# Score products of a differential attention: the low part of the queries laid out over all 128 rows

## The chip, the cores and the metric

The kernel runs on one core of a Trainium2 chip. The metric is the device time of one execution in microseconds (us). All inputs lie in HBM at the start; the result is written back to HBM. Several runs of the kernel before were timed, and one execution of it was taken apart by the hardware profiler.

## The reference

One layer of a diffusion backbone works on 512 latent tokens and 256 context tokens of width 1024: a SwiGLU half step, then a mixer (gated linear attention and differential attention side by side, gated and added), then a second SwiGLU half step and a norm. What the change touches is the differential attention of the latent tokens:

```python
def _diff_block(q, k, v, lam):
    s = jnp.einsum('bqhcd,bkhcd->bhcqk', q, k).astype(jnp.float32) * (DIFF_DH ** -0.5)
    p = jax.nn.softmax(s, axis=-1)
    a = p[:, :, 0] - lam * p[:, :, 1]
    return jnp.einsum('bhqk,bkhe->bqhe', a.astype(v.dtype), v)
```

There are 8 heads. Each has two components c = 0, 1 of width 64, and 512 queries meet 768 keys (512 latent, 256 context). Queries and latent keys are turned by an axial rotary embedding first.

## The kernel before, in words

**Number format.** A matmul here takes operands in a reduced float32 format. To keep accuracy each operand is split into a high part (`...h`, a copy in the reduced format) and a low part (`...l`, the value minus the high part). A weight product is the sum of three matmuls: high by high, high by low and low by high.

**Stages.** First SwiGLU (to about 600 us), mixer (attention to about 975 us, gated linear attention and output projection after it), second SwiGLU. The attention goes by units `un` of two heads. While unit `un - 1` attends, the projections of unit `un` are woven in: `weave` takes the generator `attend` and a list of projection calls, and after each `yield` of the one runs the next of the other. In the last unit the projections of the mixing gates (`mgate`) take that place. Before the first unit stands a prologue: the query projections of heads 0 and 1 (`gemm_lat([0, 1], G)` and `diff_q`, L664 and L665), two `mgate` calls (L666, L667), the norm of the context tokens (L668 to L671), then the keys and values of heads 0 and 1.

**Queries.** `diff_q` (L546) gets the projected queries of one head (128 rows: rows 0 to 63 are component 0, rows 64 to 127 component 1; 512 tokens along the row). `rope` leaves the rotated values in a tile of tag `t1`, of which there are two buffers; `mgate` (L472) uses the same two buffers for its result, and so does the rope of the keys. ScalarE copies them to `qh` (L551), VectorE makes `ql` (L552). Four transfers on the SyncE queue (L555) copy each 64-row half of `qh` to both halves of the rows of `QQ[:, c, :]`, so that `QQ[:, c, :]` holds the high part of component c twice. `ql` stays as it is: component c in its own 64 rows.

**Keys.** `diff_k` (L558) makes `kr` (rotated), `kh` and `kl`, and copies them (L570, L571) to `KK[:, c, :]`: the high part of component c in the rows of c, its low part in the other 64 rows.

**Scores.** `score(i)` (L602) takes 128 queries of a head. For each component c it fills one score tile `sp` of 128 x 768 in PSUM by four matmuls (L611 to L614): `ql` of component c (64 rows) against `KK[r, c]` for 512 and then 256 keys, then `QQ[:, c]` (128 rows) against `KK[:, c]` for 512 and then 256 keys. The second pair gives high by high plus high by low in one pass, the first one low by high. A head has 4 blocks of queries, so there are 8 x 4 x 2 = 64 such groups of four. After each group VectorE takes the row maximum (L615) and ScalarE the exponential (L616). `flip` transposes the weights of the block before on TensorE (L633), ScalarE and VectorE split them (L636, L637), `value` multiplies them with the values. The score tiles and the transposes share two PSUM buffers (`big`).

**What sets the order.** The kernel is written as a dataflow program; when it is compiled, a planner simulates it with costs of its own, gives each tile a buffer and fixes the order of the instructions on each engine. Each engine and the SyncE queue then run their lists strictly in that order. Loads of weights (`wload`, L109: transfer to `raw`, copy to `whi` on ScalarE, subtraction to `wlo` on VectorE or GpSimd) are traced at a higher priority and also stand on the SyncE queue. The rest of the prologue that matters: the results of `gemm_lat` lie in two PSUM buffers (`gm`), which also take the key and value projections.

Of the kernel before, what the change touches and what calls it, by code (L numbers as in the profile page):

```python
# [10 lines left out]
F32 = mybir.dt.float32  # L11
# [45 lines left out]
def layer(tc, a, out, dump=None, stop=None):  # L57
# [49 lines left out]
    loaded = [None]  # L107

    def wload(src, w=1024, eng=None, hold=None):  # L109
        """hold: the pool and number of weights that stay."""  # L110
        pl, n, wt = (*hold, w) if hold else (wp, WB, 1024)
        raw = wp.tile([P, 1024], F32, tag="raw", name=u("raw"), bufs=RB)
        hi = pl.tile([P, wt], F32R, tag="whi", name=u("whi"), bufs=n)
        lo = pl.tile([P, wt], F32R, tag="wlo", name=u("wlo"), bufs=n)
        with tc.high_priority(offset=WPRI):
            SY.dma_start(raw[:, :w], src)
            S.activation(hi[:, :w], raw[:, :w], AF.Copy)  # L117
            ld = (eng or V).tensor_tensor(lo[:, :w], raw[:, :w], hi[:, :w].bitcast(F32), op=ALU.subtract)  # L118
        loaded[0] = ld.ins
        return hi, lo  # L120
# [35 lines left out]
    class Rms:  # L156
# [4 lines left out]
        def square(self):  # L161
            """where the next squares go; the last ones are left to the sums of finish()."""
            self.c += 1
            if self.c == 1:
                return self.acc
            self.sq = self.p.tile([P, self.n], F32, tag="sq", name=u("sq"), bufs=2)
            return self.sq
# [7 lines left out]
        def add2(self, ap, ap2):  # L175
            """two token ranges; the squares of the second one are left to GpSimd."""
            n = ap.shape[-1]
            sq = self.square()
            S.activation(sq[:, :n], ap, AF.Square)
            G.tensor_tensor(sq[:, n:], ap2, ap2, op=ALU.mult)  # L180
            if 1 < self.c < KT:
                for sl in (slice(0, n), slice(n, self.n)):
                    V.tensor_tensor(self.acc[:, sl], self.acc[:, sl], sq[:, sl], op=ALU.add)

        def scale(self, start=None):
            """1/rms, tokens on the partitions."""
            nt = self.n // P
            pv = sm(u("pv"))
            with tc.issue_after(start) if start else ExitStack():
                for t in range(nt):  # L190
                    for i, q in enumerate((self.acc, self.sq)):
                        PE.matmul(pv[:, t:t + 1], q[:, t * P:(t + 1) * P], ones[:, 0:1], start=i == 0, stop=i == 1)
            v = self.p.tile([P, nt], F32, tag="rv", name=u("v"), bufs=2)
            y = self.p.tile([P, nt], F32, tag="ry", name=u("y"), bufs=2)
            V.tensor_scalar(v, pv[:, :nt], 1.0 / D, EPS, op0=ALU.mult, op1=ALU.add)
            newton(self.p, y, v, [P, nt], "nw")
            return y

        def finish(self, R, start=None, after=None):
            """R: the psum, or a function that gives the psum of a token tile.  # L200

            start: the instruction ahead of the sums; after: work ahead of R.
            """
            if not callable(R):
                R = lambda t, R=R: R[:, t * P:(t + 1) * P]
            nt = self.n // P
            y = self.scale(start)
            with tc.issue_after(after()) if after else ExitStack():
                for t in range(nt):
                    dg = self.p.tile([P, P], F32, tag="dg", name=u("dg"), bufs=3)  # L210
                    V.tensor_scalar(dg, ident, y[:, t:t + 1], None, op0=ALU.mult)
                    mm = PE.matmul(R(t), ones, dg, start=True, stop=True)
            return mm.ins

    def mod_h(pool_, x_, R, k, m, i, ai, hh, hl):
        """one feature tile of the modulated norm, as hi and lo parts."""
# [7 lines left out]
    class Parts:  # L224
        """hi (0) and lo (1) parts of feature-major tokens: latent tiles, and a tile for the context."""
# [15 lines left out]
    def mm_k(dst, w, h, k, segs):  # L241
        """the products of one feature tile; dst(o0, n): psum slice for a token segment."""
# [10 lines left out]
    class Ffn:  # L253
# [5 lines left out]
        def psum(self):  # L259
            """psum of the two up projections of one f tile: functions of a token segment."""  # L260
# [33 lines left out]
        def down(self, f0, nf, m, parts, w=None):  # L294
            """parts: (x slice, token offset, tokens, gate)."""
# [10 lines left out]
        def run(self, first, parts, extra=None):  # L306
            """all f tiles from first on and all but the last chunk of the down projection."""
# [16 lines left out]
    # ================= FFN 1 =================  # L324
# [104 lines left out]
    # last chunk of the down projection: latent tokens first, so that their norm runs under the context part  # L429
# [25 lines left out]
    # ================= mixer =================  # L455
# [4 lines left out]
    def gemm_lat(blks, eng=None):  # L460
        """128-column blocks of W_in for the latent tokens, the feature tiles outermost."""
# [7 lines left out]
    def mgate(pool_, tag, j, eng=None):  # L469
        """tanh of half of a tile of the mixing gates, kept in DRAM."""  # L470
# [9 lines left out]
    def gemm_fm(blk):  # L480
        """128 columns of W_in, feature-major: (latent psum, context psum)."""
# [7 lines left out]
    def tm_items(blk, nt, consume):  # L489
        """256 columns of W_in, token-major, two token tiles a bank: a call for each bank."""  # L490
# [40 lines left out]
    with tc.tile_pool(name="dqp", bufs=1) as dq:  # L531
# [14 lines left out]
        def diff_q(pl):  # L546
            qh = dq.tile([P, TL], F32R, tag="qh", name=u("qh"), bufs=1)
            ql = dq.tile([P, TL], F32R, tag="ql", name=u("ql"), bufs=3)
            QQ = dq.tile([P, 2, TL], F32R, tag="QQ", name=u("QQ"), bufs=3)
            qr = rope(pl, None, 0.125)  # L550
            S.activation(qh, qr, AF.Copy)  # L551
            V.tensor_tensor(ql, qr, qh.bitcast(F32), op=ALU.subtract)  # L552
            for c in range(2):
                for d in range(2):
                    SY.dma_start(QQ[d * 64:(d + 1) * 64, c, :].bitcast(F32), qh[c * 64:(c + 1) * 64, :].bitcast(F32))  # L555
            return QQ, ql

        def diff_k(blk):  # L558
# [3 lines left out]
            kl = dp.tile([P, T], F32R, tag="kl", name=u("kl"), bufs=1)  # L562
# [4 lines left out]
            V.tensor_tensor(kl, kr, kh.bitcast(F32), op=ALU.subtract)  # L567
            for c in range(2):
                r, o_ = slice(c * 64, (c + 1) * 64), slice((1 - c) * 64, (2 - c) * 64)
                SY.dma_start(KK[r, c, :].bitcast(F32), kh[r, :].bitcast(F32))  # L570
                SY.dma_start(KK[o_, c, :].bitcast(F32), kl[r, :].bitcast(F32))  # L571
            return KK

        def diff_items(un, st):
            """the projections of a pair of heads, a list of calls that fill st."""
# [22 lines left out]
        def attend(un, st):  # L598
            """attention of a pair of heads; yields where other work should follow on the tensor engine."""
            vh, vl = st["v"]  # L600

            def score(i):  # L602
                QQ, ql = st[f"q{i // 4}"]
# [4 lines left out]
                for c in range(2):  # L608
                    sp = big(u("S"))
                    r = slice(c * 64, (c + 1) * 64)  # L610
                    for n0, n1 in ((0, TL), (TL, T)):  # L611
                        PE.matmul(sp[:, n0:n1], ql[r, qs], KK[r, c, n0:n1], start=True, stop=False)  # L612
                    for n0, n1 in ((0, TL), (TL, T)):
                        PE.matmul(sp[:, n0:n1], QQ[:, c, qs], KK[:, c, n0:n1], start=False, stop=True)  # L614
# [69 lines left out]
        def head_sums(un):  # L684
            """sums of squares of the heads of a pair, tokens on the partitions."""
# [40 lines left out]
    def branch(br, j, th, yhl):  # L726
        """one feature tile of a gated branch; the second one adds to the first and is split again."""
# [14 lines left out]
    # prefix sums of the log decays (times tau), one zero ahead of each chunk  # L742
# [11 lines left out]
    # head norms of the attention output  # L754
# [18 lines left out]
    # low-rank gate: stacked hi and lo parts  # L773
# [90 lines left out]
    with tc.tile_pool(name="glp", bufs=1) as gp:  # L864
        IT = 1.0 / 16.0

        def gla_core(hd, st, tail):
# [4 lines left out]
            # factors against the states: queries (fwd, bwd), keys (fwd, bwd; latent then context)  # L872
# [43 lines left out]
            def factors(hf):  # L916
                # factors of the binary split: at half size h the two halves of a 2h block meet at its middle
# [104 lines left out]
        for hd in range(GH):  # L1022
            if hd < GH - 1:
                nst, its = gla_items(hd + 1)
            else:
                its = [lambda j=j: mgate(gi, "q", j) for j in range(10, 16)]
                its.insert(3, lambda: None)
                # the branch of the attention takes the place of the tokens
# [94 lines left out]
    # ================= FFN 2 and the final norm =================  # L1123
# [49 lines left out]
def _fm(w, n):  # L1173
    """[D, n*128] -> n blocks [128, 8*128], contraction on the partitions."""
# [3 lines left out]
def _w2(w):  # L1178
    """[FF, D] -> [128, FF*8]: by chunk of f tiles, then output tile, then f tile."""
# [8 lines left out]
def arrange(inp):  # L1188
# [40 lines left out]
    # tables that depend on shapes alone  # L1229
# [32 lines left out]
```

## Time and profile before

| what | value |
|---|---|
| median of 3 runs | 1810.89 us |
| lowest and highest run | 1808.08, 1811.19 us |
| span of the profiled execution, first to last instruction | 1809.3 us |
| TensorE busy | 1763.3 us, 97% of the span |
| VectorE, ScalarE, GpSimd busy | 1000.8, 629.8, 111.5 us |
| TensorE share of the chain that ended last | 89% |

The profile gives the profiled execution by its span; the median of the runs is 1.6 us above it. PE is TensorE's matmul side, PEld its weight-load side; matmuls overlap in the pipeline and their ends are modelled, so that the distance from one matmul's start to the next one's start says more than the duration of one. DVE is VectorE, ACT ScalarE, POOL GpSimd, SP SyncE, SPq its queue of transfers. The attention's score products run from 663 to 964 us of the span.

### The profile page before, as it was taken

What the parts mean: (1) busy time and instruction counts of PE and PEld (TensorE: products, weight loads), DVE (VectorE), ACT (ScalarE), POOL (GpSimd) and SP (SyncE); (2) the same over time, 40 slices, a digit from 0 to 9 for tenths busy, and PEclk for the clock granted to TensorE, in tenths of its full rate; (3) what the DMA queues carried; (4) which work ended last, traced back from release to release, by engine and by line L of the source; (5) the groups of instructions that cost most, each with busy time, mean ns of one, the idle gap of its engine ahead of it and who ended that gap; (6) DMA issues with size and microseconds to landing.
All of it is one profiled execution on the core that took longest, in us unless ns stands there. A gap on an engine that the chain in (4) does not pass through costs nothing.

```text
span 1809.3 us, 24815 instructions
## 1 busy us (share of the span) xinstructions
PE 1763.3 (97%) x10184; PEld 1525.2 (84%) x10184; DVE 1000.8 (55%) x1666; ACT 629.8 (35%) x940; POOL 111.5 (6%) x190
## 2 busy tenths in 40 slices
PE   6999999999999999999999989999999999999998
PEld 4788888888888788888877889998888988888887
DVE  5554354354445856766655675767645743333435
ACT  3321121121113435555565543434423332222233
POOL 3100000000001300000000031212001200000000
PEclk9999999999999999999999899999999999999999
DMA  8333344243333532312222121112444222323231
GB/s 327 138 117 98 114 157 131 73 160 121 107 117 105 156 94 74 101 54 76 94 70 90 33 70 56 39 47 94 157 148 142 89 82 93 105 83 110 87 110 66
DMA packets 59426, 189.42 MB, mean 105 GB/s; under 512 B 7976, under 2 KB 8232, under 8 KB 58032
## 3 DMA queue, kind: packets, MB, share of 16 engines
q1 hardware_dynamic: 59312, 187.83, 32.2%
q8 instruction: 80, 1.31, 0.3%
q14 instruction: 34, 0.28, 0.0%
HBM read 168.93 MB, written 8.39 MB: 98 GB/s over the span
## 4 chain that ended last, share of the span: by engine, by line
PE 89%; DVE 3%; ACT 1%; issue 1%; DMA 1%; POOL 1%; DVEq 0%; ACTq 0%; POOLq 0%
PE h L249 21%; PE h L246 11%; PE pl L249 8%; PE dn L123 5%; PE dn L124 5%; PE dn L125 5%; PE pl L246 4%; PE pb L249 3%; PE ptm L504 3%; PE ptm L505 3%; PE ptm L506 3%; PE S L614 2%; PE S L612 2%; PE po L249 2%; PE pb L246 1%; PE pc L249 1%
## 5 line engine op out<-in xcount | busy, mean ns | idle before, releaser
L117 ACT ACTIVATE whi<-raw 128x1024 fp32r<-128x1024 f32 (+2 forms) x246 | 241.2, 984 | 505.9 <-PE dn L125 191.6
L118 DVE TENSOR_TENSOR wlo<-raw,whi 128x1024 fp32r<-128x1024 f32 (+2 forms) x231 | 262.2, 1137 | 220.7 <-ACT whi L117 219.2
L246 PE MATMUL h<-hH,wlo 128*128 128x512 f32 (+1 forms) x704 | 273.3, 388 | 1.9 <-ACT hH L221 1.4
L249 PE MATMUL h<-hL,whi 128*128 128x512 f32 (+1 forms) x704 | 274.5, 390 | 0.6 <-DVE hL L222 0.6
L249 PE MATMUL h<-hH,whi 128*128 128x512 f32 (+1 forms) x704 | 273.2, 388 | 0.0
L249 PE MATMUL h<-hC,whi 128*128 128x256 f32 x704 | 196.9, 280 | 0.0
L123 PE MATMUL dn<-gh,wlo 128*128 128x512 f32 (+1 forms) x568 | 194.5, 343 | 1.1 <-ACT gh L286 0.9
L124 PE MATMUL dn<-gl,whi 128*128 128x512 f32 (+1 forms) x568 | 194.1, 342 | 0.0
L125 PE MATMUL dn<-gh,whi 128*128 128x512 f32 (+1 forms) x568 | 193.6, 341 | 0.0
L246 PEld LDWEIGHTS h<-hH,wlo 128*128 128x128 f32 x704 | 132.2, 188 | 33.3 <-ACT hH L221 2.4
L249 PEld LDWEIGHTS h<-hH,whi 128*128 128x128 f32 x704 | 132.3, 188 | 29.6
L249 PEld LDWEIGHTS h<-hL,whi 128*128 128x128 f32 x704 | 132.2, 188 | 28.0 <-DVE hL L222 0.8
L246 PE MATMUL pl<-hH,wlo 128*128 128x512 f32 x328 | 132.2, 403 | 7.8 <-DVE sg L839 4.7
L285 DVE TENSOR_TENSOR g<-s,h 128x512 f32<-128x512 f32 (+2 forms) x46 | 36.2, 791 | 182.4 <-PE h L249 110.0
L249 PEld LDWEIGHTS h<-hC,whi 128*128 128x128 f32 x704 | 133.0, 189 | 0.6 <-DVE hC L222 0.4
L249 PE MATMUL pl<-hL,whi 128*128 128x512 f32 x328 | 130.9, 399 | 0.0
L249 PE MATMUL pl<-hH,whi 128*128 128x512 f32 x328 | 130.3, 397 | 0.0
L123 PEld LDWEIGHTS dn<-gh,wlo 128*128 128x128 f32 x568 | 107.6, 189 | 14.2 <-ACT gh L286 1.1
L125 PEld LDWEIGHTS dn<-gh,whi 128*128 128x128 f32 x568 | 107.5, 189 | 12.4
L124 PEld LDWEIGHTS dn<-gl,whi 128*128 128x128 f32 x568 | 107.6, 190 | 12.2
L505 PE MATMUL ptm<-wlo,hH 128*128 128x256 f32 x384 | 110.5, 288 | 5.0 <-DVE wlo L118 5.0
L504 PE MATMUL ptm<-whi,hL 128*128 128x256 f32 x384 | 111.9, 292 | 0.0
(269 smaller groups left out, 3339.9 us busy)
## 6 DMA issues: line engine op xcount, KB each, us to landing
raw<-win SPq DMA_DIRECT2D x65, 512.0 KB, 3.6
adaw<-ada SPq DMA_DIRECT2D x56, 512.0 KB, 4.4
raw<-f1w SPq DMA_DIRECT2D x44, 512.0 KB, 3.6
raw<-f2w SPq DMA_DIRECT2D x44, 512.0 KB, 3.5
aw<-ada SPq DMA_DIRECT2D x8, 1024.0 KB, 10.0
raw<-wbr SPq DMA_DIRECT2D x16, 512.0 KB, 3.9
raw<-f1w SPq DMA_DIRECT2D x16, 384.0 KB, 3.1
raw<-wout SPq DMA_DIRECT2D x12, 512.0 KB, 3.5
```

The lines of the kernel that those rows point to most:

```text
L117: S.activation(hi[:, :w], raw[:, :w], AF.Copy)
L118: ld = (eng or V).tensor_tensor(lo[:, :w], raw[:, :w], hi[:, :w].bitcast(F32), op=ALU.subtract)
L123: PE.matmul(out_, wl, xh, start=first, stop=False)
L124: PE.matmul(out_, wh, xlo, start=False, stop=False)
L125: PE.matmul(out_, wh, xh, start=False, stop=last)
L246: PE.matmul(dst(o0, n), wl[:, ks], h.at(0, k, o0, n), start=(k == 0), stop=False)
L249: mm = PE.matmul(dst(o0, n), wh[:, ks], h.at(i, k, o0, n), start=False, stop=(k == KT - 1 and i == 0))
L285: self.mark = V.tensor_tensor(g[:, sl], s[:, sl], pts[1][:, sl], op=ALU.mult).ins
L504: PE.matmul(o_, tl, wh[:, cs], start=f, stop=False)
L505: PE.matmul(o_, th, wl[:, cs], start=False, stop=False)
L506: PE.matmul(o_, th, wh[:, cs], start=False, stop=l)
L612: PE.matmul(sp[:, n0:n1], ql[r, qs], KK[r, c, n0:n1], start=True, stop=False)
```

## The change

The low part of the queries gets the layout that the high part has. `QQ` grows by a dimension: `QQ[:, 0, c]` holds the high part of component c in both halves of the rows, `QQ[:, 1, c]` the low part in both halves. Eight transfers instead of four fill it. All four matmuls of a score group now use 128 rows; the first pair therefore adds low by low to the product, which the kernel before left out. The low part is made in place in the rotated tile (`qr`), that of the keys in `kr`, so that `ql` (three buffers) and `kl` (one buffer) fall away; the transfers read the low parts from `qr` and `kr`. Comments and docstrings were also emptied, line for line.

```diff
         def diff_q(pl):
             qh = dq.tile([P, TL], F32R, tag="qh", name=u("qh"), bufs=1)
-            ql = dq.tile([P, TL], F32R, tag="ql", name=u("ql"), bufs=3)
-            QQ = dq.tile([P, 2, TL], F32R, tag="QQ", name=u("QQ"), bufs=3)
+            QQ = dq.tile([P, 2, 2, TL], F32R, tag="QQ", name=u("QQ"), bufs=3)
             qr = rope(pl, None, 0.125)
             S.activation(qh, qr, AF.Copy)
-            V.tensor_tensor(ql, qr, qh.bitcast(F32), op=ALU.subtract)
-            for c in range(2):
-                for d in range(2):
-                    SY.dma_start(QQ[d * 64:(d + 1) * 64, c, :].bitcast(F32), qh[c * 64:(c + 1) * 64, :].bitcast(F32))
-            return QQ, ql
+            V.tensor_tensor(qr, qr, qh.bitcast(F32), op=ALU.subtract)
+            for i, src in enumerate((qh.bitcast(F32), qr)):
+                for c in range(2):
+                    for d in range(2):
+                        SY.dma_start(QQ[d * 64:(d + 1) * 64, i, c, :].bitcast(F32),
+                                     src[c * 64:(c + 1) * 64, :])
+            return QQ
...
-            kl = dp.tile([P, T], F32R, tag="kl", name=u("kl"), bufs=1)
...
-            V.tensor_tensor(kl, kr, kh.bitcast(F32), op=ALU.subtract)
+            V.tensor_tensor(kr, kr, kh.bitcast(F32), op=ALU.subtract)
...
-                SY.dma_start(KK[o_, c, :].bitcast(F32), kl[r, :].bitcast(F32))
+                SY.dma_start(KK[o_, c, :].bitcast(F32), kr[r, :])
...
-                    r = slice(c * 64, (c + 1) * 64)
-                    for n0, n1 in ((0, TL), (TL, T)):
-                        PE.matmul(sp[:, n0:n1], ql[r, qs], KK[r, c, n0:n1], start=True, stop=False)
-                    for n0, n1 in ((0, TL), (TL, T)):
-                        PE.matmul(sp[:, n0:n1], QQ[:, c, qs], KK[:, c, n0:n1], start=False, stop=True)
+                    for q in (1, 0):
+                        for n0, n1 in ((0, TL), (TL, T)):
+                            PE.matmul(sp[:, n0:n1], QQ[:, q, c, qs], KK[:, c, n0:n1], start=q == 1, stop=q == 0)
```

## Rows read from the trace of the kernel before

**Rows 1.** The page, busy time of each engine, share, instructions.

```profile
PE 1763.3 (97%) x10184; PEld 1525.2 (84%) x10184; DVE 1000.8 (55%) x1666; ACT 629.8 (35%) x940; POOL 111.5 (6%) x190
```

**Rows 2.** Windows, attention: length, busy of PE, PEld, DVE, ACT, POOL, clock, DMA.

```profile
662.70:965.00 302.30, 302.30 (x1785) 250.49 (x1784) 202.87 (x303) 165.89 (x269) 0.00 (x0) 1.00 0.27 79
```

**Rows 3.** Waits, 655 to 970 us: total us, times, longest.

```profile
DVE st L615 <- PE S L614: 38.9, 30, 3.3
```

**Rows 4.** Timeline of PE around a score group: start, length, instruction, rows*columns, shape, count.

```profile
704.33 0.28 PE L506 MATMUL ptm<-whi,hC 128*128 128x256 f32 x1
704.54 0.62 PE L612 MATMUL S<-KK,ql 64*128 64x512 f32 x2
705.09 0.61 PE L614 MATMUL S<-KK,QQ 128*128 128x512 f32 x2
705.54 0.28 PE L504 MATMUL ptm<-whi,hC 128*128 128x256 f32 x1
```

**Rows 5.** Timeline of PEld for the same group; idle time before in brackets.

```profile
705.09 0.30 PEld L614 LDWEIGHTS S<-KK,QQ 128*128 128x128 f32 x2 [0.25 <-issue]
705.43 0.19 PEld L504 LDWEIGHTS ptm<-whi,hC 128*128 128x128 f32 x1
```

**Rows 6.** Timeline of PE in the first SwiGLU, all of 128 rows.

```profile
100.25 0.40 PE L246 MATMUL h<-hH,wlo 128*128 128x512 f32 x1
100.48 0.28 PE L246 MATMUL h<-hC,wlo 128*128 128x256 f32 x1
100.60 0.39 PE L249 MATMUL h<-hL,whi 128*128 128x512 f32 x1
```

**Rows 7.** Lines 612 and 614: counts, ns min/median/max, first and last start; idle before 614.

```profile
L612 PE MATMUL S<-KK,ql x128: 271/384/501, 663.0 to 963.6; 64*128 64x512 f32 x64, 64*128 64x256 f32 x64
...
  issue: 15.9, 64
```

**Rows 8.** Timeline of DVE, the split of the transposes ahead of that group.

```profile
703.37 0.95 DVE L637 TENSOR_TENSOR al<-aT,ah 128x768 fp32r<-128x768 f32 x1
```

**Rows 9.** Tile QQ: its transfers (ns of the issue), and us from issue to landing.

```profile
L555 SPq DMA_DIRECT2D QQ<-qh x32: 461/593/882, 620.0 to 877.6; - x32
...
DMA to landing us min/median/max: 2.2/2.9/4.2
```

**Rows 10.** The rope's tile t: an addition in place, and the subtraction to ql.

```profile
L543 DVE TENSOR_TENSOR t<-t,sw x8: 678/686/693, 618.6 to 874.4; 128x512 f32<-128x512 f32 x8
...
L552 DVE TENSOR_TENSOR ql<-t,qh x8: 682/683/686, 620.4 to 875.9; 128x512 fp32r<-128x512 f32 x8
```

**Rows 11.** Timeline of the SP queue in the prologue.

```profile
620.05 2.43 SPq L555 DMA_DIRECT2D QQ<-qh  x4
622.58 0.53 SPq L116 DMA_DIRECT2D raw<-win  x1
...
624.93 2.38 SPq L555 DMA_DIRECT2D QQ<-qh  x4
```

**Rows 12.** Timeline of ACT in the prologue.

```profile
621.73 0.60 ACT L473 ACTIVATE mg<-pl 128x512 f32<-128x512 f32 x1 [1.71 <-PE pl L249]
...
624.28 0.63 ACT L551 ACTIVATE qh<-t 128x512 fp32r<-128x512 f32 x1 [1.00 <-DMA QQ<-qh]
628.21 0.60 ACT L473 ACTIVATE mg<-pl 128x512 f32<-128x512 f32 x1 [3.31 <-PE pl L249]
```

**Rows 13.** Timeline of PE in the prologue: the first key projection.

```profile
628.38 0.48 PE L246 MATMUL pl<-hH,wlo 128*128 128x512 f32 x1
...
630.29 0.31 PE L246 MATMUL pc<-hC,wlo 128*128 128x256 f32 x1
```

**Rows 14.** Timeline of the SP queue behind the third query projection.

```profile
678.57 0.51 SPq L116 DMA_DIRECT2D raw<-win  x1
```

**Rows 15.** Timeline of ACT: where that load is taken up.

```profile
707.90 1.06 ACT L117 ACTIVATE whi<-raw 128x1024 fp32r<-128x1024 f32 x1 [0.17 <-PE ptm L506]
```

**Rows 16.** Windows, the start of the gated linear attention; columns as in Rows 2.

```profile
992.00:999.50 7.50, 7.50 (x22) 5.37 (x22) 4.67 (x8) 2.89 (x4) 0.21 (x2) 0.54 0.25 72
```

More of the change, by code (lines that the diff above doesn't have):

```diff
@@ L602, in score @@
             def score(i):
-                QQ, ql = st[f"q{i // 4}"]
+                QQ = st[f"q{i // 4}"]
                 KK = st[f"k{i // 4}"]
```

## The prediction

> **What bounds the kernel now.** I read the page's busy times first: TensorE is busy for 97% of the span and VectorE, the next, for 55% [rows 1]. Then the attention alone, because the change lies there: in the 302.3 us from the first score group to the last, PE is busy all the time, VectorE 203 us and ScalarE 166 us, at full clock [rows 2]. The list of waits of that stretch has nobody that PE waits for; its long rows are engines that wait for PE, such as the row maximum, 38.9 us on the scores [rows 3]. So a microsecond saved on PE here is a microsecond of the kernel, until another engine becomes late.
>
> But busy is not working. Matmul ends are modelled, so I read starts, on the timeline. With 128 rows throughout, a matmul of 512 columns is followed by the next start after 0.23 us and one of 256 columns after 0.12 us [rows 6]. A score group has 2 x (512 + 256) columns, hence 2 x 0.35 = 0.70 us by that step. What it takes is more: the 256-column matmul ahead starts at 704.33, the 64-row pair at 704.54, the 128-row pair at 705.09, the next projection matmul at 705.54 [rows 4]. That is 1.21 us where 0.12 + 0.70 = 0.82 us would do: 0.39 us too much. It comes in two equal halves. Entering the 64-row pair costs 0.21 instead of 0.12 (0.09 over), the pair 0.55 instead of 0.35 (0.20 over; 0.09 to 0.10 of this is again the change of shape at its end, the rest lies inside it), and the 128-row pair 0.45 instead of 0.35 (0.10 over). The weight loads show why the pairs themselves are long: a load normally starts about 0.11 us ahead of its matmul (705.43 for the matmul at 705.54), but the first load after a change of shape starts with its matmul, at 705.09, after 0.25 us in which the load side did nothing and waited for nothing that the profile shows [rows 4, 5]. So each change between 64 and 128 rows empties the array (0.09 to 0.10 us) and then exposes one weight load (0.10 to 0.11 us), and each group has two changes.
>
> **What the change takes away.** There are 128 matmuls of 64 rows, two a group, thus 64 groups, and the idle stretch ahead of the 128-row pair occurs 64 times, 15.9 us in all, 0.25 us each: the pattern holds in every group, not in the one shown alone [rows 7]. With 128 rows everywhere no change of shape is left in the attention. The added rows cost nothing: a matmul's step follows its columns (0.35 us for 512 + 256 at 128 rows [rows 6]; the 64-row pair is not shorter than the 128-row pair even with one exposed load taken off each [rows 4]). The term is 64 x 0.39 = 25.0 us; with 0.38 and 0.41 for the rounding of the starts it is 24.3 to 26.2 us.
>
> The Trainium skill, TensorEngine Tiling (Array Packing), section Key Properties, says that changing the tiling mode drains the TensorE, and says nothing of the weight load behind it. The trace agrees on the drain (0.09 us) and adds the exposed load. By the drain alone the term would be half; that is a rival below.
>
> **What becomes late next.** In a faster stretch the tightest hand-over is a PSUM buffer: the second score group of a block takes the buffer of the transposes, which VectorE clears in a split that ends at 703.37 + 0.95 = 704.32, and the group starts at 704.54, 0.22 us later [rows 4, 8]. Without the empty time the group wants to start 0.09 us sooner, and its first load 0.11 us before that, 0.20 us in all. The chain in front of the split starts with the first score group, whose end moves along, so little is lost: zero below, 32 blocks x 0.1 us = 3.2 us above. I take 0.5 us, because rows like this leave a remainder of 0.02 us.
>
> **What it adds.** (1) Subtractions in place. An addition in place of the same shape with float32 output took 686 ns, the subtraction to `ql` 683 ns [rows 10]: 8 x 3 ns, and as much for the keys, on an engine with a third of the stretch free. I take nothing, with +/- 0.1 us as bounds.
>
> (2) 32 more transfers, four for each of the 8 query tiles, of 0.59 us on the SP queue each, landing 2.9 us after issue [rows 9]: 2.4 us more of SP a time. They wait for the subtraction, 0.7 us after the copy, while SP is still issuing the first four (2.4 us), so that SP hardly waits. Behind them on SP stand weight loads. In the steady part such a load is issued at 678.57 and taken up at 707.90 [rows 14, 15]; 2.4 us of 29 us are hidden, and nothing is lost. The scores don't wait either: heads 0 and 1 would have their low parts by 624.93 + 2.38 + 0.5 + 2.4 + 2.9 = 633 us, the first score is at 663.0 [rows 7, 11].
>
> (3) The prologue is where the cover is thin. The rotated queries now stay in a `t1` buffer until their last copy has landed, and the first `mgate` result takes the same buffer at 621.73, 1.7 us after the first four transfers began [rows 11, 12]. With four more transfers and one weight load on SP between, head 0's buffer is free at about 622.48 + 0.53 + 2.4 + 2.9 = 628.3 us, 6.6 us later. What waits for this `mgate` result is the PSUM buffer of the first key projection, which starts at 628.38 [rows 13]: some 0.6 us late (tanh 0.60 us [rows 12]). The second one moves likewise, and its PSUM buffer is wanted only by the value projection behind the key projection. If the planner puts the late tanh behind the query copy of head 1 on ScalarE, this is all; if it keeps the order, it is rival C. The loads move by 2.4 us while the queue is crowded, which can delay ScalarE's list by about as much. Bounds: 0 and 9 us (C's price below); I take 1.0 us, near the lower end, because the planner sees when a buffer comes free.
>
> (4) Outside the attention nothing changes but the moment at which things happen. At the start of the gated linear attention the granted clock falls to half for a while (0.54 of full over 992.0 to 999.5 us [rows 16]). Such a stretch costs at most 7.5 x 0.46 = 3.5 us, and whether one falls more or less often after a shift can't be read from here: 0 +/- 3.5 us, which is about the spread of the three runs (3.1 us).
>
> **Sum.** The profiled execution has a span of 1809.3 us: 1809.3 - 25.0 + 0.5 + 1.0 = 1785.8 us. The median of the runs is 1.6 us above the span, so 1787.4 us.
>
> **Rivals.**
> A (forecast): both drains and both exposed loads go. 1787.4 us; with the bounds above, without C, -1.2 - 1.5 - 3.5 and +0.7 + 2.7 + 3.5 us, rarely together: 1782 to 1793 us. Chance 0.70.
> B: the drains go, but the loads stay exposed, because the score's load hangs on a semaphore and can't be pulled ahead for that reason. Then 64 x 0.19 = 12.2 us go: 1809.3 - 12.2 + 1.5 + 1.6 = 1800.2 us. For it: only score groups pair the two symptoms in these rows. Against it: the load ahead of the 128-row pair shows no releaser, just issue [rows 5, 7]. The drain rule of the page named above would come out here. 0.08.
> C: ScalarE keeps its order in the prologue. The first tanh comes at 628.3 instead of 621.7; the query copy of head 1 (624.28) stands behind it and comes at 628.9; its eight transfers end at 628.9 + 0.6 + 4.8 = 634.3 and land at 637.2, which makes the second tanh 9.0 us late (628.21). Behind that are the weights and the context norm that PE needs from 630.29 on [rows 11 to 13]. PE loses up to 9 us instead of 1: 1795.4 us. Against it: the order is planned anew for the changed program. 0.14.
> D (slower): the low parts come late for each head: PE, in order, waits at the first score of each of the 8 query tiles for four more issues and a landing, 4 x 0.59 + 2.9 = 5.3 us, 42 us in all: 1787.4 + 42 = 1829 us. It decides as soon as the copies land after the score asks, and is slower than before from 3.2 us a time on. Against it: 30 us to spare for heads 0 and 1 as worked out under (2). 0.04, which also holds a worse order from the planner.
> E: the 0.39 us are not from the change of shape but a hand-over of PSUM, so they stay: 1809.3 + 1.5 + 1.6 = 1812.4 us. Against it: they are alike in 64 groups, whatever stands ahead. 0.04.
>
> **Chances and range.** A measurement here tells 0.2% (3.6 us) from no change. A, B and C are all faster by more: 0.92. E gives no change, 0.04; D slower, 0.04. The range 1782 to 1796 us takes in A and most of C, 0.82.
>
> **What would show it.** In the changed trace: the score pairs 0.35 us apart, 1.21 us down to about 0.82 us from neighbour to neighbour; score loads starting about 0.1 us ahead of their matmuls; no idle stretch on PEld ahead of scores; the stretch of the scores 302 - 25 = 277 us long with PE busy throughout; 64 transfers to QQ. Wrong would be: steps of 0.45 us inside pairs (B), an idle PE between 622 and 640 us (C), PE waiting at scores for transfers (D), a step that stays at 1.21 us (E), or a large gain or loss outside 600 to 970 us.

## The result, and the profile after

The changed kernel takes 1787.43 us (median of four runs, 1785.35 to 1789.07) against 1810.43 us for the kernel before (1808.08 to 1811.19): a ratio of 0.9878, 95% interval 0.9866 to 0.9889. The forecast was 1787.4 us, range 1782 to 1796. The profiled execution was the fastest of the four, with a span of 1783.6 us in a run of 1785.35 us; so its span lies 3.8 us below the median, and not all of its difference to the span before (25.7 us) belongs to the change.

The score groups first. Timeline of PE in the changed kernel, around a group among projections (start, length, instruction, shape, count):

```profile
745.10 0.28 PE L249 MATMUL pc<-hC,whi 128*128 128x256 f32 x1
745.22 0.86 PE L613 MATMUL S<-KK,QQ 128*128 128x512 f32 x4
745.91 0.39 PE L249 MATMUL pl<-hH,whi 128*128 128x512 f32 x1
```

From the 256-column matmul ahead to the one behind it is 0.81 us, where the kernel before took 1.21 us for the same columns [rows 4]; the entry takes 0.12 us instead of 0.21. The four matmuls now stand in one row of the timeline, because there is no gap between the two pairs. The weight loads of the same group:

```profile
745.10 0.65 PEld L613 LDWEIGHTS S<-KK,QQ 128*128 128x128 f32 x4
745.79 0.19 PEld L249 LDWEIGHTS pl<-hH,whi 128*128 128x128 f32 x1
```

The first load of the group starts at 745.10, 0.12 us ahead of its matmul; the idle stretch of 0.25 us in front of the 128-row pair [rows 5, 7], which the kernel before had 64 times, is gone.

Where the time went by stage. Windows of the kernel before, cut at the first and at the last score group (length, busy time and count of PE, PEld, DVE, ACT, POOL, granted clock, DMA share, GB/s):

```profile
600.00:662.80 62.80, 59.69 (x361) 52.43 (x359) 39.53 (x70) 22.00 (x33) 10.86 (x6) 1.00 0.44 132
662.80:962.90 300.10, 300.10 (x1775) 249.13 (x1774) 201.21 (x302) 165.76 (x269) 0.00 (x0) 1.00 0.27 80
962.90:1060.00 97.10, 87.98 (x506) 76.24 (x505) 61.09 (x120) 49.16 (x71) 12.58 (x31) 0.88 0.17 52
```

The same cuts in the changed kernel:

```profile
600.00:662.76 62.76, 59.38 (x355) 51.98 (x355) 39.11 (x70) 21.75 (x33) 10.35 (x6) 1.00 0.51 149
662.76:940.49 277.73, 277.73 (x1775) 249.12 (x1774) 200.52 (x302) 164.74 (x269) 0.00 (x0) 1.00 0.34 97
940.49:1040.00 99.51, 89.97 (x544) 78.87 (x543) 64.74 (x128) 50.07 (x73) 12.84 (x32) 0.90 0.18 59
```

The stretch of the scores went from 300.1 to 277.7 us with the same 1775 matmuls, and PE is busy in all of it in both: 22.4 us, of which the busy share says nothing. The cut stands ahead of the last group, which gives another 0.4 us, so the scores brought 22.8 us. Up to the first score group the two differ by 0.04 us; as the first SwiGLU ended 0.5 us earlier in this execution (the first query projection starts at 602.0 instead of 602.5 us), the prologue lost about 0.5 us. The remaining 2.9 us of the span's difference come after the attention, where the change touches nothing. By starts of equal instructions, 2.0 us of them arise between 965 and 1060 us of the span before, around the stretches of reduced clock, and 0.9 us in two places later on. The medians are 23.0 us apart, close to the 22.3 us that scores and prologue give together.

### The profile page after: what moved, and what is told of

It is laid out like the page before. It is cut to its first block, busy times and chain, and to the rows that moved or that the text cites. A ratio compares the mean times of both kernels' runs of the same rounds, so it can differ in the third digit from the quotient of the medians.

```text
span 1783.6 us, 24883 instructions
## 1 busy us (share of the span) xinstructions
PE 1738.2 (97%) x10184; PEld 1523.1 (85%) x10184; DVE 1000.3 (56%) x1666; ACT 629.1 (35%) x940; POOL 111.6 (6%) x190
## 4 chain that ended last, share of the span: by engine, by line
PE 89%; DVE 3%; ACT 1%; issue 1%; POOL 1%; DMA 1%; DVEq 0%; ACTq 0%; POOLq 0%
PE h L249 22%; PE h L246 11%; PE pl L249 8%; PE dn L123 5%; PE dn L124 5%; PE dn L125 5%; PE pl L246 4%; PE pb L249 3%; PE ptm L505 3%; PE ptm L504 3%; PE ptm L506 3%; PE S L613 3%; PE po L249 2%; PE pb L246 1%; PE pa L956 1%; PE pc L249 1%
```

## The experiments

Theory 1 is the forecast's: on the tensor engine each change between 64 and 128 rows costs about 0.2 us, a part of it for emptying the array and a part for a weight load that isn't hidden. Each kernel below ran beside the kernel before on the same chip.

**Everything but the 128 rows.**

```diff
                     for q in (1, 0):
+                        r = slice(c * 64, (c + 1) * 64) if q else slice(0, P)
                         for n0, n1 in ((0, TL), (TL, T)):
-                            PE.matmul(sp[:, n0:n1], QQ[:, q, c, qs], KK[:, c, n0:n1], start=q == 1, stop=q == 0)
+                            PE.matmul(sp[:, n0:n1], QQ[r, q, c, qs], KK[r, c, n0:n1], start=q == 1, stop=q == 0)
```

> The changed kernel with everything kept (eight copies for each query tile, low parts in place) except that the low-part products read only the 64 rows of their component again. Theory 1 (each change between 64 and 128 rows on the tensor engine costs about 0.2 us, two changes a group): the whole gain goes, 1787.4 + 22.5 = 1810 us, 1806 to 1813; the steps of a group are back at 0.55 and 0.45 us. Rival 2 (the gain comes from the rest of the change: low parts that arrive by transfer, fewer tiles, another order): it stays at 1787 us, 1784 to 1790.

Measured: 1810.71 us against 1811.77 us, ratio 0.9996 (0.9986 to 1.0005). The whole gain is gone, with the eight transfers and the subtractions in place still there. So what they cost or save lies within 2.5 us gained and 0.9 us lost (the interval), and rival 2 falls. Timeline of PE in this kernel:

```profile
713.65 0.39 PE L246 MATMUL pl<-hH,wlo 128*128 128x512 f32 x1
713.97 1.16 PE L614 MATMUL S<-KK,QQ 64*128 64x512 f32 x4
714.97 0.40 PE L249 MATMUL pl<-hL,whi 128*128 128x512 f32 x1
```

The group is back at 1.32 us from neighbour to neighbour, behind a matmul of 512 columns (0.23 + 0.70 = 0.93 would do: 0.39 too much).

**Half of the groups.** The slice is 64 rows for component 1 alone:

```diff
...
+                        r = slice(c * 64, (c + 1) * 64) if q and c else slice(0, P)
...
```

> The changed kernel with 64-row low products for component 1 alone, 128 rows for component 0: 32 of the 64 groups change shape. Theory 1: half of the gain, 1787.4 + 11.3 = 1798.7 us, 1796 to 1802. Rival 2: 1787 us. A rival by which one shape anywhere in the stretch slows all of it: 1810 us.

Measured: 1798.4 us against 1811.77 us, ratio 0.9926 (0.9909 to 0.9943): 13.4 us (10.3 to 16.5 by the interval), by 32 of 64 groups; the whole change brings 23.0 us by the medians above and 24.7 us in its repeat below. The gain follows the number of changes.

**96 rows.**

```diff
...
+                        r = slice(0, 96) if q else slice(0, P)
...
```

> The changed kernel with low-part products over rows 0 to 95 instead of 0 to 127 (leaves out part of the low parts' products). Theory 1a (what costs is to change the way the array is divided, and 96 rows run undivided as 128 do): 1787 us, 1784 to 1790, steps of 0.35 us in the groups. Theory 1b (any change of the number of rows costs): 1810 us, 1806 to 1813.

Measured: 1788.46 us, ratio 0.9869 (0.9854 to 0.9883). Timeline of PE in this kernel:

```profile
710.98 0.39 PE L246 MATMUL pl<-hH,wlo 128*128 128x512 f32 x1
711.21 0.86 PE L614 MATMUL S<-KK,QQ 96*128 96x512 f32 x4
711.91 0.40 PE L249 MATMUL pl<-hL,whi 128*128 128x512 f32 x1
```

0.93 us from neighbour to neighbour, as if nothing changed: theory 1b falls, 96 rows run beside 128 at no cost. So not every change of the number of rows costs: 96 beside 128 is free, 64 beside 128 is not. That the array runs 64 rows in another division, and 96 in the same one as 128, is theory 1a's reading; it fits, but no run shows the division itself.

**Twice the changes.** In the kernel before, the two pairs are interleaved:

```diff
                     for n0, n1 in ((0, TL), (TL, T)):
                         PE.matmul(sp[:, n0:n1], ql[r, qs], KK[r, c, n0:n1], start=True, stop=False)
-                    for n0, n1 in ((0, TL), (TL, T)):
                         PE.matmul(sp[:, n0:n1], QQ[:, c, qs], KK[:, c, n0:n1], start=False, stop=True)
```

> The kernel before with the four matmuls of a group in the order low 512, high 512, low 256, high 256: the same matmuls, but four changes of shape a group instead of two. Theory 1 (a price for each change, 0.19 to 0.20 us): 64 x 2 x 0.195 = 25 us more, 1810.4 + 25 = 1835 us, 1830 to 1839. Rival 3 (the price belongs to each 64-row matmul, or once to each group): no change, 1810 us, 1807 to 1814.

Measured: 1836.97 us against 1811.77 us, ratio 1.0132 (1.0113 to 1.015): 25.2 us more by the medians, 23.9 us by the ratio, with the very same matmuls in another order. Rival 3 falls. Timeline of PE in this kernel:

```profile
717.32 0.39 PE L246 MATMUL pl<-hH,wlo 128*128 128x512 f32 x1
717.64 0.49 PE L612 MATMUL S<-KK,ql 64*128 64x512 f32 x1
718.06 0.50 PE L613 MATMUL S<-KK,QQ 128*128 128x512 f32 x1
718.49 0.38 PE L612 MATMUL S<-KK,ql 64*128 64x256 f32 x1
718.80 0.39 PE L613 MATMUL S<-KK,QQ 128*128 128x256 f32 x1
719.03 0.39 PE L249 MATMUL pl<-hL,whi 128*128 128x512 f32 x1
```

From 717.32 to 719.03 is 1.71 us for columns that take 0.93 us: 0.78 us for four changes, 0.195 us each, the price of two changes doubled.

**The changed kernel again, beside the three below.**

> The changed kernel itself, beside the three below on the same chip: 1787.4 us, 1785 to 1790, ratio to the kernel before 0.988.

Measured: 1786.79 us (1784.69 to 1788.72) against 1811.45 us, ratio 0.9868 (0.9853 to 0.9883).

**128 rows by zeros, without the copies.** Three fixed tiles `QL` whose other halves are cleared once:

```diff
...
+            for c in range(2):
+                r = slice(c * 64, (c + 1) * 64)
+                V.tensor_tensor(QL[r, c, :], qr[r, :], qh[r, :].bitcast(F32), op=ALU.subtract)
...
+                    for w in (QL, QQ):
                         for n0, n1 in ((0, TL), (TL, T)):
-                            PE.matmul(sp[:, n0:n1], QQ[:, q, c, qs], KK[:, c, n0:n1], start=q == 1, stop=q == 0)
+                            PE.matmul(sp[:, n0:n1], w[:, c, qs], KK[:, c, n0:n1], start=w is QL, stop=w is QQ)
...
```

> The low parts of the queries padded with zeros to 128 rows in three fixed tiles, written in place there by two subtractions of 64 rows; no copies of the low part, four transfers for each query tile as before the change. Theory 1 and the accounting of the changed trace (0.5 us of PE lost in the prologue to the rearranged list and the late weights behind the copies; copies cost nothing later): 1787 us, up to 0.5 us less than the changed kernel, at worst 1 us more through 8 more subtractions of 0.69 us on VectorE. A rival by which the eight copies cost a microsecond each: 1779 us.

Measured: 1786.80 us, ratio 0.9872 (0.9855 to 0.989), the same as the changed kernel. The 128 rows win, not what is in them, and the copies don't cost a microsecond each. From the first query projection to the first score group this kernel takes 0.7 us longer than the changed kernel's repeat (61.5 against 60.7 us), the scores behind it 0.3 us less. PE in this kernel, at the first `mgate` projection:

```profile
623.27 0.39 PE L249 MATMUL pl<-hH,whi 128*128 128x512 f32 x1
625.46 0.47 PE L246 MATMUL pl<-hH,wlo 128*128 128x512 f32 x1 [1.81 <-DVE t L541]
```

and in the changed kernel:

```profile
620.80 0.39 PE L249 MATMUL pl<-hH,whi 128*128 128x512 f32 x1
621.99 0.47 PE L246 MATMUL pl<-hH,wlo 128*128 128x512 f32 x1 [0.79 <-DVE t L540]
```

The wait for VectorE's rope of head 1 grew by 1.0 us; the second subtraction of head 0, 0.69 us, now stands ahead of this rope.

**The same at another place.** After the attention the head norms (`head_norm`, L767) spread 8 scales over the rows by matmuls of 8 rows. Their operands are padded with zeros to 128 rows:

```diff
-    selb = gi.tile([P, 12, P], F32R, tag="v", name="selb", bufs=2)[0:8]
-    V.tensor_copy(selb[:, 0:8, :], selb_)
+    selb = gi.tile([P, 12, P], F32R, tag="v", name="selb", bufs=2)
+    G.memset(selb[:, 0:8, :].bitcast(F32), 0.0)
+    V.tensor_copy(selb[0:8, 0:8, :], selb_)
...
+    for t in (rh, rl_):
+        G.memset(t.bitcast(F32), 0.0)
...
```

> The changed kernel with the head norms of the attention output (16 matmuls of 8 rows among projections of 128 rows, after the attention) padded with zeros to 128 rows. Theory 1 carried to another place: at most 2 changes of shape around each of 8 pairs, in the trace of the changed kernel about 0.1 to 0.3 us each: 1 to 3 us less than the changed kernel, 1785 us. If the stretch of half clock that starts in these matmuls goes too, up to 3.4 us more: 1781 us. Rival: the row count there doesn't matter, since nothing is won where the clock is low anyway: 1787 us.

Measured: 1782.30 us (1780.91 to 1783.43), ratio 0.9845 (0.9831 to 0.9859): 4.5 us below the changed kernel of the same session, with no run of the one inside the runs of the other. The rival's 1787 us falls; the time lies between the 1785 us of theory 1 and the 1781 us with the stretch of half clock, which the repeat's trace doesn't have there either (clock 1.00 from 968.1 to 985 us). It beats both kernels. Timeline of PE in the changed kernel's repeat, around the first two head norms:

```profile
968.18 0.39 PE L249 MATMUL pl<-hH,whi 128*128 128x512 f32 x1
968.50 0.50 PE L768 MATMUL Rd<-ryl,selb 8*128 8x512 f32 x1
968.84 0.39 PE L769 MATMUL Rd<-ryh,selb 8*128 8x512 f32 x1
969.07 0.39 PE L768 MATMUL Rd<-ryl,selb 8*128 8x512 f32 x1
969.31 0.38 PE L769 MATMUL Rd<-ryh,selb 8*128 8x512 f32 x1
969.62 0.50 PE L790 MATMUL z<-lrs,w2h 128*128 128x512 f32 x1
969.96 0.28 PE L791 MATMUL z<-lrs,w2h 128*128 128x256 f32 x1
```

and with zeros to 128 rows:

```profile
966.63 0.39 PE L249 MATMUL pl<-hH,whi 128*128 128x512 f32 x1
966.86 0.39 PE L771 MATMUL Rd<-ryl,selb 128*128 128x512 f32 x1
967.09 0.39 PE L772 MATMUL Rd<-ryh,selb 128*128 128x512 f32 x1
967.32 0.40 PE L771 MATMUL Rd<-ryl,selb 128*128 128x512 f32 x1
967.55 0.40 PE L772 MATMUL Rd<-ryh,selb 128*128 128x512 f32 x1
967.82 0.48 PE L793 MATMUL z<-lrs,w2h 128*128 128x512 f32 x1
```

An excursion to 8 rows costs the same as one to 64: 0.09 us to enter, 0.11 us for the first load, 0.08 and 0.11 us on the way back (968.18 to 969.96 is 1.78 us, six matmuls of 0.23 are 1.38). The matmuls in between, all of 8 rows, keep the step of 0.23 us. There are six such excursions in the repeat's trace, 2.3 us by this price.

The spans of the two profiled executions are 3.8 us apart. By starts of equal instructions, 1.5 us of this arise in the first 50 us of the execution, where the edit touches nothing, 1.9 us in the stretch of the six excursions (in which the kernel with zeros waits 0.5 us for other things) and 0.3 us behind it. So about 2 us are seen to come from the rows; the rest of the 4.5 us between the medians isn't settled.

**Both.**

> Both of the two above together, zero padding of the low parts of the queries and of the head norms: 1784.5 us, 1780 to 1787 us, below the changed kernel if either of them wins anything.

Measured: 1783.17 us, ratio 0.985 (0.9834 to 0.9866): the same as the head norms alone, 3.6 us below the kernel with zeros for the queries alone, and within the range.

## Why the prediction was right

**Drain and exposed load, 64 groups.** Right in mechanism, shown by four doses: no change of shape left (ratio 0.9878), half of them (0.9926), all of them (0.9996), twice as many (1.0132). The starts of the first and the last score matmul lie 301.1 us apart in the kernel before, and 278.4, 289.1, 301.1 and 325.4 us in these four; with 96 rows it is 278.5 us. So the time goes and comes back in the scores. The price per group was read as 0.39 us; it is 0.39 us back again in the kernel with 64 rows and 0.78 us with four changes.

That the price is 0.09 us of drain and 0.11 us of exposed load is read from the starts; no run takes away the one without the other. Rival B, by which the loads stay exposed, falls all the same: the group shown above takes 0.69 us from its first matmul to the one behind it, where rival B would have 2 x 0.45 us, and its loads run ahead. In the 27 groups that stand right behind the transposes the first pair does take 0.43 us, but the way into it only 0.03 us; from the last transpose to the second pair it is 0.46 us, where rival B would have 0.12 + 0.45 = 0.57 us. The Trainium skill (TensorEngine Tiling (Array Packing), Key Properties) says that a change of the tiling mode drains the TensorE. The trace agrees with 0.09 us on entering; the load behind it makes up the other half of the price.

**What became late next.** Here the size was off. The forecast set 25.0 - 0.5 = 24.5 us for the scores; they brought 22.8 us, so 2.2 us were lost where 0.5 us was taken. Some 0.9 us of it is a hand-over of PSUM buffers: ten groups of the changed trace are 0.04 to 0.19 us late in it. In four of them VectorE's split clears the buffer last, as the forecast had it; in the other six it is ScalarE's exponential, which reads the score tile that stood there, and the three latest groups are among these. In the one shown here the exponential ends at 683.37 + 0.19 = 683.56, the first load follows at 683.61, and from the matmul ahead to the one behind it is 1.01 us instead of 0.82. PE, ACT and PEld in the changed kernel:

```profile
683.41 0.28 PE L506 MATMUL ptm<-whi,hH 128*128 128x256 f32 x1
683.61 0.96 PE L613 MATMUL S<-KK,QQ 128*128 128x512 f32 x4
684.42 0.28 PE L504 MATMUL ptm<-whi,hL 128*128 128x256 f32 x1
683.37 0.19 ACT L615 ACTIVATION_READ_ACCUMULATOR e<-S,st 128x1 f32 x1
683.61 0.64 PEld L613 LDWEIGHTS S<-KK,QQ 128*128 128x128 f32 x4
```

The rest is a wait that the forecast didn't name. Waits of 655 to 970 us in the changed kernel (total us, times, longest):

```profile
PEld o L123 <- ACT ah L635: 2.1, 7, 0.5
PEld S L613 <- DVE al L636: 0.2, 1, 0.2
```

The products with the values (`o`) now reach the head of PE's list before ScalarE has split the transposes. One of the seven, the longest (0.46 us at 949 us), lies behind the last score group, and the kernel before has it there too; the other six, 1.7 us, are new. By the distances of the matmuls' starts PE loses about 1 us in these six. Hand-over and this wait together are some 2 us; the bound of 3.2 us, worked out for the hand-over alone, happens to cover both.

**Transfers.** 32 more were counted; the changed kernel has 32 copies of the low part, issued in 596 ns at the median, and with 64-row products all of them together make no difference (0.9996). That SP would hardly wait for the subtraction holds in the prologue. SP queue of the changed kernel:

```profile
619.55 2.44 SPq L556 DMA_DIRECT2D QQ<-qh  x4
622.03 2.52 SPq L556 DMA_DIRECT2D QQ<-t  x4
624.64 2.48 SPq L556 DMA_DIRECT2D QQ<-qh  x4
627.22 2.46 SPq L556 DMA_DIRECT2D QQ<-t  x4
```

**The prologue.** 1.0 us was taken, about 0.5 us was lost. The planner did what the forecast leaned on: the first tanh waits for head 0's copies and stands behind the query copy of head 1 now. ACT of the changed kernel:

```profile
623.79 0.63 ACT L551 ACTIVATE qh<-t 128x512 fp32r<-128x512 f32 x1 [1.46 <-DMA QQ<-qh]
626.41 0.60 ACT L473 ACTIVATE mg<-pl 128x512 f32<-128x512 f32 x1 [1.99 <-DMA QQ<-t]
...
633.25 0.60 ACT L473 ACTIVATE mg<-pl 128x512 f32<-128x512 f32 x1
```

The tanh came 4.7 us later (626.41 against 621.73 [rows 12]), the second one 5.0 us later. The forecast had 6.6 us: the copies began 0.5 us sooner, the weight load didn't stand between them (0.5 us), and the last copy landed 1.9 us after its issue had ended, where 2.9 us were added. Neither tanh held PE, so the 0.6 us of the forecast's late key projection didn't occur: that projection starts at 627.91 us, 0.5 us sooner than before, like all around it. Rival C, the old order, did not occur. What PE did lose is a wait for late weights in the value projection:

```profile
627.91 0.48 PE L246 MATMUL pl<-hH,wlo 128*128 128x512 f32 x1
...
638.03 0.28 PE L504 MATMUL ptm<-whi,hL 128*128 128x256 f32 x1
638.59 0.39 PE L505 MATMUL ptm<-wlo,hH 128*128 128x256 f32 x1 [0.28 <-DVE wlo L118]
```

From 638.03 to 638.59 is 0.56 us where 0.12 would do. The same wait of 0.44 us stands in the 64-row variant, so it doesn't belong to the rows; the kernel with zeros, which has no copies of the low part, is without it, though it also reaches this place 0.4 us later.

**Clock and sum.** For the reduced clock 3.5 us either way were left open. That this was the right size can't be told from the spread of the runs alone (spans of 1783.6 to 1787.3 us), but two profiled executions of the changed kernel show it in part: behind the last score group the repeat is 2.1 us shorter than the first one, and its granted clock over 980 to 1060 us is 0.91 against 0.89. Ahead of the mixer the repeat is 1.8 us longer at a clock of 1.00, so runs differ by other things too. That the median met the forecast to 0.1 us is luck: the gain at the scores was set 1.7 us too high, the loss in the prologue 0.5 us too high, and runs differ by more than that.

Two figures of the prediction are off, and no term of the sum rests on them. The longest row in the list of waits [rows 3] isn't an engine that waits for PE but ScalarE's exponential, which waits 79.7 us for VectorE's row maximum. And rival D would have been slower than the kernel before from (1810.9 - 1787.4) / 8 = 2.9 us a time on, not from 3.2 us.

## What to carry to other kernels

In a stretch bound by the tensor engine look at the distance between starts of neighbouring matmuls, not at busy time: an engine that was busy 100% of the stretch gave back 7.5% of it. A few products over 64 or 8 rows, scattered among 128-row products, cost 0.39 us an excursion here, at full clock; filling the operands up to 128 rows (a copy or zeros) takes this away without making the products longer, as long as the data gets there beside other work. Where such products must stay, put them next to each other, and count the changes of shape before choosing the order of an accumulation.

## What the runs showed of the hardware that was not expected

Products of 96 rows mixed with products of 128 rows cost nothing (0.93 us for the group and its neighbour, 1788.46 us), products of 8 rows cost an excursion like those of 64 (0.39 us), and four 8-row products in a row keep the full step of 0.23 us. Row counts other than 8, 64, 96 and 128 were not run.
